# A layer step on one core: 56 instead of 48 tokens of the expert layer by row, one of its one-hots on ScalarE, and the second norm in two sets of columns

## The chip, the cores and the metric

The kernel is one program on one core of a Trainium2 chip. The metric is device time in microseconds (us), the median of repeated runs. The engines are named as the profile names them: PE (TensorE), DVE (VectorE), ACT (ScalarE), POOL (GpSimd), SP (the engine that issues the weight loads).

## The reference, cut to what matters

One layer of a decoder on 264 tokens (256 of a prompt and one each of 8 samples), all in fp32. The change lies in the second half of it, from `x1` on:

```
q   = x1 @ w_q                                  # 8 heads x 2 x 128
s1, s2 = q[:, :, 0] . keys1, q[:, :, 1] . keys2 # 128 scores each
t1, i1 = top_k(s1, 16);  t2, i2 = top_k(s2, 16)
cand = t1[:, None] + t2[None, :]                # 256 per head
top, pos = top_k(cand, 16); idx = i1 * 128 + i2 at pos
gate = softmax(top)                             # 8 x 16 = 128 experts per token
hid  = gelu(x1 . u_tab[idx])                    # 16,384 experts of 2,048 numbers
peer = sum(gate * hid * v_tab[idx])
x2   = LN(ALPHA * x1 + peer)
y    = x2 + sigmoid(x2 @ ple_gate_w) * (p @ ple_proj_w)
```

## The kernel before, in words

**Two ways through the expert layer.** A token needs 128 rows of `u_tab` and of `v_tab`. `NSP` tokens (the last ones, the samples among them) are done by row: for each, 128 rows of `uR` are gathered by an indirect DMA into a tile `ug` of 128 x 2048 (1 MiB), DVE multiplies them with the token's `x1` and sums (L1230), then 128 rows of `vR` are gathered and added with their coefficients into a sum tile `x1s` (L1240). All other tokens, `TD` = 264 - `NSP` = 216, are done densely by PE: all 16,384 experts' products with `x1` (stage U, 128 blocks of two weight halves), a gelu, a multiplication with a gate matrix that is zero where an expert was not chosen, and the sum over all experts (stage V, 8 chunks of 16 blocks).

**A block on PE.** `pair_block` (L261 to L278) takes two weight tiles of 128 x 1024 (a "half" each). A weight is split by ACT into a rounded part `whi` (`split_w`, L146) and by DVE into the rest `wlo` (L147). Per slice of 128 rows there are two matmuls: `whi` with the activations' two parts beside each other (2·TD columns, L271 or L274) and `wlo` with the first part alone (TD columns, L272). So 16 pairs make a block. The stages ahead use `col_block`, three matmuls of 264 columns per slice (L235 to L237); the change does not touch them.

**What sets the order.** All five instruction streams are written out by hand. Each half is a `tick`: the weight fetch four halves ahead is issued on SP (five `w` buffers, L135), the split three halves ahead is put on ACT and DVE (four `whi` and `wlo` buffers), the half's matmuls are issued, and then the background gets a budget of about one microsecond of DVE time (`background`). Background work is a list of generators that yield the cost of what they just issued, or a wait of n ticks; what stands earlier in the list is served first. The engines then run these streams first-in first-out, held by semaphores only. The generators here:

- `select` (L1020) finds the 16 best of each head, in three token sets t = 0, 1, 2; `select_all` (L1088) runs them and starts what follows.
- `gates` (L1152) makes the gate matrix: per group of 4 tokens POOL writes a one-hot with the gate in it, `o1` (4 x L1165), DVE writes a plain one-hot `o2` (L1166), PE multiplies the two six ticks later (`g_mm`, L1178), ACT copies the product into `gs` (L1179), SP sends `gs` to DRAM. A grid asks for 3 ticks from group to group.
- `sparse_experts` (L1194) does the tokens by row in groups `GR` of 32 and 16. One job is one gather and one DVE pass; a gather is issued one job ahead, and a grid asks for `STEP` = 4 ticks from job to job. For a group of n tokens, `x1s` first takes 128/n copies of the group's `x1` rows (L1220) and later the sum, which PE folds at the end (L1246).
- `prep` (L1305) makes the dense coefficients for V: it loads gates and products (`gl`, `al`, issued on POOL), multiplies them on DVE (L1315, L1316) and splits the result on ACT and DVE (`co`, L1324, L1325). Each chunk of 16 blocks needs four such steps; a chunk begins with `run_out`, which issues at once what is left of them.
- `Norm` (L800) gathers the second norm's sums while the last chunk of V still runs: every evacuated block (L1351, L1354) gets the tokens by row copied in (POOL, L1355) and is then treated over all 264 columns (L825, L831, L832, L841 to L844). `n2` is this norm. The projection behind it (`ple_half`, 16 blocks of `w_pg`) follows.

## Time and profile before

| | before |
|---|---|
| median of 3 runs | 2614.34 us (2608.11 to 2621.4) |
| the profiled execution | 2611.91 us, span 2610.1 us |
| PE busy | 2579.9 us (99%) |
| DVE, ACT, POOL busy | 2033.3, 1342.6, 734.4 us |
| moved by DMA | 676.77 MB |

In time, the part up to `x1` ends near 1147 us; stage U runs from there to 1850 us, V to 2495 us, the projection behind it to the end. A row of the profile names line, engine and operation, then what is written and read (`out<-in`), its shape and a count; "idle before" is time in which that engine stood still just ahead of it, with the instruction that ended the wait. A row of a timeline begins with its start and its duration in us.

### The profile page before, as it was taken

How to read it: one execution, taken by the hardware profiler on the slowest of the kernel's cores; microseconds unless marked ns; L12 is line 12 of the kernel's file. 1: busy time of each engine (PE TensorE's matmuls, PEld its weight loads, DVE VectorE, ACT ScalarE, POOL GpSimd, SP SyncE). 2: the span in 40 equal slices, each digit the busy share in tenths (PEclk: the TensorE clock that was granted, in tenths of full speed). 3: DMA queues.
4: the chain of work that ended last, by engine and by line, in shares of the span. 5: the costliest groups of instructions: out<-in, count | busy, mean ns of one | idle time of the engine just before them, and what ended most of it. 6: DMA issues, size and time to landing. Idle time of an engine off the chain costs nothing.

```text
span 2610.1 us, 48704 instructions
## 1 busy us (share of the span) xinstructions
PE 2579.9 (99%) x18967; PEld 2526.5 (97%) x18967; DVE 2033.3 (78%) x3256; ACT 1342.6 (51%) x1893; POOL 734.4 (28%) x774
## 2 busy tenths in 40 slices
PE   9999999999999999999999999999999999999999
PEld 8999999999999999999999999999999999999999
DVE  8899965556445567889998777778889799897886
ACT  5665533444334444655556655656445444444563
POOL 2232200000000010100269999883322232220100
PEclk9999999999999999999999999999999999999999
DMA  7798755656666666667778999899999999997664
GB/s 236 220 302 271 240 178 176 181 175 181 184 179 179 183 180 179 177 184 209 227 228 316 351 331 337 332 335 391 366 360 378 346 370 371 373 379 232 202 199 133
DMA packets 201399, 676.77 MB, mean 259 GB/s; under 512 B 23168, under 2 KB 60704, under 8 KB 187680
## 3 DMA queue, kind: packets, MB, share of 16 engines
q1 hardware_dynamic: 156384, 509.65, 59.9%
q0 software_dynamic: 26768, 145.43, 14.8%
q10 hardware_dynamic: 18016, 18.58, 2.0%
q8 instruction: 148, 2.42, 0.4%
q14 instruction: 83, 0.68, 0.1%
HBM read 632.67 MB, written 40.90 MB: 258 GB/s over the span
## 4 chain that ended last, share of the span: by engine, by line
PE 90%; DVE 4%; DMA 4%; issue 1%; ACT 0%; SPq 0%; POOL 0%; DVEq 0%; POOLq 0%; ACTq 0%
PE mm L271 26%; PE mm L237 15%; PE mm L235 15%; PE mm L236 15%; PE mm L272 14%; DMA w<-uT 2%; PE mm L274 2%; PE gps L1178 2%; DVE wlo L147 1%; DVE x1s L1240 1%; DMA al<-a_d 0%; DMA ug<-vR,sidx 0%; ACT whi L146 0%; DMA ug<-uR,sidx 0%; PE scr L996 0%
## 5 line engine op out<-in xcount | busy, mean ns | idle before, releaser
L147 DVE TENSOR_TENSOR wlo<-w,whi 128x1024 fp32r<-128x1024 f32 x916 | 1120.4, 1226 | 392.1 <-ACT whi L146 388.8
L146 ACT CAST whi<-w 128x1024 fp32r<-128x1024 f32 x916 | 960.2, 1050 | 797.2 <-PE mm L236 287.4
L271 PE MATMUL mm<-x,whi 128*128 128x432 f32 x1920 | 607.1, 373 | 0.7 <-ACT whi L146 0.7
L271 PE MATMUL mm<-co,whi 128*128 128x432 f32 x1920 | 601.9, 371 | 3.5 <-DVE co L1325 3.5
L237 PE MATMUL mm<-x,wlo 128*128 128x264 f32 x1920 | 549.3, 286 | 2.8 <-DVE wlo L147 2.8
L235 PE MATMUL mm<-x,whi 128*128 128x264 f32 x1920 | 549.0, 286 | 0.1
L236 PE MATMUL mm<-x,whi 128*128 128x264 f32 x1920 | 546.6, 285 | 0.0
L272 PE MATMUL mm<-x,wlo 128*128 128x216 f32 x2048 | 519.1, 264 | 7.6 <-DVE wlo L147 7.6
L272 PE MATMUL mm<-co,wlo 128*128 128x216 f32 x2048 | 518.4, 263 | 3.3 <-DVE wlo L147 3.3
L272 PEld LDWEIGHTS mm<-x,wlo 128*128 128x128 f32 x2048 | 391.4, 191 | 13.4 <-DVE wlo L147 11.3
L272 PEld LDWEIGHTS mm<-co,wlo 128*128 128x128 f32 x2048 | 390.5, 191 | 6.0 <-DVE wlo L147 4.3
L271 PEld LDWEIGHTS mm<-co,whi 128*128 128x128 f32 x1920 | 361.6, 188 | 21.9 <-DVE co L1325 5.1
L271 PEld LDWEIGHTS mm<-x,whi 128*128 128x128 f32 x1920 | 361.9, 188 | 16.5 <-ACT whi L146 0.9
L1165 POOL TENSOR_SCALAR o<-iot,slot,slot 128x128 f32<-128x128 f32 x216 | 360.2, 1676 | 24.3 <-PE gps L1178 20.7
L237 PEld LDWEIGHTS mm<-x,wlo 128*128 128x128 f32 x1920 | 361.7, 188 | 3.2 <-DVE wlo L147 3.2
L235 PEld LDWEIGHTS mm<-x,whi 128*128 128x128 f32 x1920 | 362.8, 189 | 1.8 <-issue 1.4
L236 PEld LDWEIGHTS mm<-x,whi 128*128 128x128 f32 x1920 | 362.9, 189 | 0.0
L1202 POOL DMA_INDIRECT ug<-vR,sidx x48 | 84.4, 1759 | 292.7 <-DVE x1s L1240 218.7
L833 POOL CAST r1h<-r1gbh 128x2 fp32r<-128x2 f32 x16 | 5.2, 326 | 476.3 <-PE mm L237 476.3
L1230 DVE SCALAR_TENSOR_TENSOR ug<-ug,x1s 128x2048 f32<-128x2048 f32 x48 | 109.7, 2286 | 10.8 <-DMA ug<-uR,sidx 10.8
L1240 DVE SCALAR_TENSOR_TENSOR x1s<-ug,scf,x1s 128x2048 f32<-128x2048 f32 x46 | 107.9, 2345 | 2.6 <-DMA ug<-vR,sidx 2.6
L1202 POOL DMA_INDIRECT ug<-uR,sidx x48 | 70.5, 1468 | 116.7 <-DVE ug L1230 106.0
(350 smaller groups left out, 3834.6 us busy)
## 6 DMA issues: line engine op xcount, KB each, us to landing
w<-uT SPq DMA_DIRECT2D x256, 512.0 KB
w<-vP SPq DMA_DIRECT2D x256, 512.0 KB
w<-w_in SPq DMA_DIRECT2D x240, 512.0 KB
w<-w_bc SPq DMA_DIRECT2D x32, 512.0 KB
w<-w_bs SPq DMA_DIRECT2D x32, 512.0 KB
w<-w_o SPq DMA_DIRECT2D x32, 512.0 KB
w<-w_q SPq DMA_DIRECT2D x32, 512.0 KB
w<-w_pg SPq DMA_DIRECT2D x32, 512.0 KB
```

What stands on the lines that cost most here:

```text
L146: ac.copy(hi, w)
L147: ve.tensor_tensor(lo, w, hi.bitcast(F), OP.subtract)
L235: te.matmul(ps, wh, xh[kb], start=(first and q == 0), stop=False)
L236: te.matmul(ps, wh, xl[kb], start=False, stop=False)
L237: te.matmul(ps, wl, xh[kb], start=False, stop=(last and q == n - 1))
L271: te.matmul(ps, hi[:, ws], xp[kb], start=(kb == 0), stop=False)
L272: te.matmul(ps[:, :TD], lo[:, ws], xp[kb][:, :TD], start=False, stop=False)
L274: te.matmul(ps, hi[:, ws], xp[kb], start=False, stop=True)
L1165: gp.tensor_scalar(o1[:, q], iot, slot[0][:, c], slot[2][:, c], OP.is_equal, OP.mult)
L1202: gp.indirect_dma_start(out=t, out_offset=None, in_=tab, in_offset=bass.IndirectOffsetOnAxis(ap=sidx[:, c:c + 1], axis=0))
L1230: ve.scalar_tensor_tensor(t, t, 1.0, x1s, OP.mult, OP.mult, accum_out=shid[:, c:c + 1])
L1240: ve.scalar_tensor_tensor(x1s, t, scf[:, c:c + 1], x1s, OP.mult, OP.add)
```

## The change

- `NSP` is 56, so `TD` is 208, and `GR` gets a third group of 8 tokens. `NB`, `TR` (gates kept in blocks of 32 tokens and a rest) follow: the rest is 16 tokens instead of 24.
- `o2` comes from ACT: per group four `Abs` of (slot - iota) and one `Relu` of (1 - that) over all four, where DVE had one `is_equal`.
- `sparse_experts` starts after set t = 1 and at the head of the task list, where it started after t = 0 and at its end. Jobs come every 4 ticks, but every second one (every fourth in V) after 3. `x1s` has two buffers; the next group's copies come by one DMA (`replicate`) while the present group is in its second half, and the fold is a task of its own (`folded`).
- `select` works through its one-hot search in quarters instead of halves.
- `prep` is put at the head of the list and waits 2 instead of 3 ticks between steps; the budget of a tick in V is 1.1 instead of 1.0.
- The second norm gathers only the dense columns of each block (`w` = TD). The columns of the tokens by row are done for all 16 blocks at once (`finish`, `Norm.rest`), when the last fold is through.

```diff
-NSP = 48
+NSP = 56
-GR = ((0, 32), (32, 16))
+GR = ((0, 32), (32, 16), (48, 8))
...
     class Norm:
-        def __init__(self, g_base, b_base, name, new):
+        def __init__(self, g_base, b_base, name, new, w=T):
...
-            ve.tensor_tensor(s, s, self.c, OP.subtract)
+            ve.tensor_tensor(s[:, :w], s[:, :w], self.c[:, :w], OP.subtract)
...
+        def rest(self, xs, sq):
+            w, n = self.w, T - self.w
+            ps = bank("pil")
+            te.matmul(ps[:, :n], o128, xs[:, 0], start=True, stop=True)
+            c = block("pc")[:, :n]
+            ac.copy(c, ps[:, :n])
+            yield ("w", 1)
+            ve.tensor_tensor(xs, xs, c[:, None, :].to_broadcast([128, 16, n]), OP.subtract)
...
+            ac.activation(sq, xs, AF.Square)
+            ve.tensor_reduce(self.acc[0][:, w:T], xs.rearrange("p j t -> p t j"), AX.X, OP.add)
...
+            ve.tensor_reduce(self.acc[1][:, w:T], sq.rearrange("p j t -> p t j"), AX.X, OP.add)
+            yield 1.0
+            for j in range(16):
+                while len(self.h) <= j:
+                    yield ("w", 1)
+                h, l, x = self.h[j][:, w:T], self.l[j][:, w:T], xs[:, j]
+                ac.activation(h, x, AF.Copy, scale=col(self.g, j))
+                gp.tensor_copy(self.d[j][:, w:T], x)
+                def low(h=h, l=l, x=x, j=j):
+                    ve.scalar_tensor_tensor(l, x, col(self.g, j), h.bitcast(F), OP.mult, OP.subtract)
+                soon(low)
+                yield 0.2
...
-        HH = max(1, nh // 2)
+        HH = max(1, nh // 4)
...
-            if t == 0:
-                spawn(sparse_experts())
+            if t == 1:
+                spawn(sparse_experts(), True)
...
-            ve.tensor_tensor(o2, iot[:, None, :].to_broadcast([128, 4, 128]),
-                             slot[1][:, tt:tt + 4, None].to_broadcast([128, 4, 128]), OP.is_equal)
+                ac.activation(o2[:, q], iot, AF.Abs, bias=slot[1][:, c], scale=-1.0)
+            ac.activation(o2, o2, AF.Relu, bias=1.0, scale=-1.0)
...
+        def replicate(g):
+            k0, n = GR[g]
+            t = lp.tile([128, D], F, name="x1s", tag="x1s", bufs=2)
+            gp.dma_start(out=t, in_=bass.AP(tensor=x1_d.tensor, offset=x1_d.offset + k0 * D,
+                                            ap=[[0, 128 // n], [D, n], [1, D]]))
+            return t
...
             if tab is uR and c == k0:
-                x1s = lp.tile([128, D], F, name="x1s", tag="x1s", bufs=1)
-                for q in range(128 // n):
-                    gp.dma_start(out=x1s[q * n:(q + 1) * n], in_=x1_d[ks])
-                yield ("w", 4)
+                x1s = xr
...
             get(i + 1)
-            yield grid(STEP)
+            yield grid(STEP - (i % (4 if vp else 2) == 0))
...
             if c == ECH - 1:
-                s = a[:, :T]
                 ve.tensor_tensor(a[:, :TD], a[:, :TD], a[:, TD:], OP.add)
-                gp.tensor_copy(s[:, TD:], x1sp[:, db])
-                n2.add(s)
+                n2.add(a[:, :T])
...
-            while "sparse" not in DONE:
-                tick(1.1)
-            spawn(ple_parts())
+            spawn(finish())
         co = [CO.pop(16 * c + e) for e in range(16)]
         for db in range(KB):
-            pair_block(co, v_evac(c, db), 1.0)
+            pair_block(co, v_evac(c, db), 1.1)
```

What this does to the order is seen best at three places. The first is ACT's stream in the middle of the gates (stage U), one gate group's worth of it. Before, with `as` the evacuated products, `gs` the gate matrix and `whi` the next weight:

```order
L1280 COPY as<-mm 128x216
L146 CAST whi<-w 128x1024
L1179 COPY gs<-gps 128x4x128
L1284 ACTIVATE as<-as 128x432
L1285 DMA a_d<-as 128x432
L146 CAST whi<-w 128x1024
```

And after, at the corresponding place:

```order
L1332 COPY as<-mm 128x208
L1201 ACTIVATE o_17359<-iot,slot_14374 128x128 x4
L1202 ACTIVATE o_17359<-o_17359 128x512
L146 CAST whi<-w 128x1024
L1336 ACTIVATE as<-as 128x416
L1337 DMA a_d<-as 128x416
L146 CAST whi<-w 128x1024
L1332 COPY as<-mm 128x208
L146 CAST whi<-w 128x1024
L1214 COPY gs<-gps 128x4x128
```

Five instructions per group have come onto ACT between the weight splits (the `o` tile is `o2`); no further table loads stand between them.

The second place is DVE's stream at the end of a chunk of V, 752 weight splits (L147) into the program. Before:

```order
L147 TENSOR_TENSOR wlo<-w,whi 128x1024
L1315 TENSOR_TENSOR al<-al,gl 128x4x192
L1316 TENSOR_TENSOR al<-al,gl 128x4x24
L147 TENSOR_TENSOR wlo<-w,whi 128x1024
L1351 TENSOR_TENSOR acc<-mm,acc 128x432
L1230 SCALAR_TENSOR_TENSOR ug,shid<-ug,x1s 128x2048
L1325 TENSOR_TENSOR co<-al,co 128x4x216
L147 TENSOR_TENSOR wlo<-w,whi 128x1024
L1230 SCALAR_TENSOR_TENSOR ug,shid<-ug,x1s 128x2048
L147 TENSOR_TENSOR wlo<-w,whi 128x1024
```

After, at the same count:

```order
L147 TENSOR_TENSOR wlo<-w,whi 128x1024 x2
L1403 TENSOR_TENSOR acc<-mm,acc 128x416
L1299 SCALAR_TENSOR_TENSOR x1s<-ug,scf,x1s 128x2048
L147 TENSOR_TENSOR wlo<-w,whi 128x1024 x2
L1403 TENSOR_TENSOR acc<-mm,acc 128x416
```

The chunk's last step of `prep` stood right at the chunk's end, together with two jobs by row; now the four steps stand closer together early in the chunk and are over by its end.

The third is DVE's stream in the last chunk, 869 splits in, where `Norm.rest` (L863, L867, L870) is woven between the blocks' own norm work:

```order
L1405 TENSOR_TENSOR acc<-acc 128x208
L829 TENSOR_TENSOR acc<-acc,pc 128x208
L863 TENSOR_TENSOR x1sp<-x1sp,pc 128x896
L147 TENSOR_TENSOR wlo<-w,whi 128x1024
L845 SCALAR_TENSOR_TENSOR r_28332<-acc,cpar,r_28332 128x208
L847 TENSOR_TENSOR da<-da,acc 128x208
L848 TENSOR_TENSOR dsq<-dsq 128x208
L867 TENSOR_REDUCE da<-x1sp 128x56
```

Before, the same norm instructions stood there with 264 columns, and nothing of a rest. By the same count, the first job by row stands 441 splits in (460 before) and the last 859 (820 before); the last evacuation of V is at 883 in both.

More of the change, by code (lines that the diff above doesn't have):

```diff
@@ L187, in background, with spawn @@
                 clock["credit"] -= r
-    def spawn(gen):
+    def spawn(gen, first=False):
         tk = {"gen": gen, "wait": 0}
-        tasks.append(tk)
+        tasks.insert(0 if first else len(tasks), tk)
         return tk
@@ L200, in __call__ @@
         def __call__(self, n):
-            self.t = max(self.t + n, clock["t"] + 1)
+            self.t = max(self.t + n, clock["t"])
             return ("w", self.t - clock["t"])
@@ L817, in pilot @@
             ps = bank("pil")
-            te.matmul(ps[:, :T], o128, self.s0, start=True, stop=True)
+            te.matmul(ps[:, :self.w], o128, self.s0[:, :self.w], start=True, stop=True)
             self.c = block("pc")
-            ac.copy(self.c, ps[:, :T])
+            ac.copy(self.c[:, :self.w], ps[:, :self.w])
             self.gather(self.s0)
@@ L830, in on_act @@
             def on_act():
-                ac.activation(h[:, :T], s, AF.Copy, scale=col(self.g, j))
-                ac.activation(q, s, AF.Square)
+                ac.activation(h[:, :w], s[:, :w], AF.Copy, scale=col(self.g, j))
+                ac.activation(q[:, :w], s[:, :w], AF.Square)
                 gp.tensor_copy(h[:, T:], self.gb[0][:, j])
@@ L1138, in send @@
                 src = range(lo, min(lo + m, n))
-                rows(gp, g, 0, src, m * m, 128 // m, m)
+                if len(src):
+                    rows(gp, g, 0, src, m * m, 128 // m, m)
         else:
@@ L1144, in later_rows @@
                 for h in range(PH):
-                    rows(sy, g, h * m + m - NS, range(h * NS, h * NS + NS), m * m, 1, m)
+                    rows(sy, g, h * TOPK + m - NS, range(h * NS, h * NS + NS), m * m, TOPK // m, m)
                 DONE["sent"] = True
@@ L1209, in index, with folded @@
             gp.dma_start(out=scf[:, k0:k0 + n], in_=sg_d[g])
+        def replicate(g):
[4 more added lines that the diff above has]
+            return t
+        def folded(g, acc):
+            k0, n = GR[g]
+            yield ("w", 2)
+            ps = bank("yS")
+            for db in range(KB):
+                te.matmul(ps[:, db * n:(db + 1) * n], acc[:, db * 128:(db + 1) * 128], fld[:, k0:k0 + n],
+                          start=True, stop=True)
+                if db % 4 == 3:
+                    yield ("w", 1)
+            xs = x1sp[:, :, k0:k0 + n]
+            ve.scalar_tensor_tensor(xs, xs, ALPHA, ps[:, 0:KB * n].rearrange("p (j t) -> p j t", t=n),
+                                    OP.mult, OP.add)
+            yield 0.8
+            DONE["S" + str(g)] = True
         yield ("w", 1)
@@ L1213, in sparse_experts @@
         get(0)
+        xr = replicate(0)
+        yield ("w", 4)
         grid = Grid()
+        g = 0
         for i, (tab, k0, n, c) in enumerate(jobs):
@@ L1217, in sparse_experts @@
             if tab is uR and c == k0:
-                x1s = lp.tile([128, D], F, name="x1s", tag="x1s", bufs=1)
-                for q in range(128 // n):
-                    gp.dma_start(out=x1s[q * n:(q + 1) * n], in_=x1_d[ks])
-                yield ("w", 4)
-            if i == 32:
-                while "sent" not in DONE:
+                x1s = xr
+            if tab is vR and c == k0 and g + 1 < len(GR):
+                while g + 1 == len(GR) - 1 and "sent" not in DONE:
                     yield ("w", 1)
-                index(1)
+                index(g + 1)
+                xr = replicate(g + 1)
             get(i + 1)
-            yield grid(STEP)
+            yield grid(STEP - (i % (4 if vp else 2) == 0))
             t = rows.pop(i)
@@ L1242, in sparse_experts @@
             if c == k0 + n - 1:
-                yield ("w", 2)
-                ps = bank("yS")
-                for db in range(KB):
-                    te.matmul(ps[:, db * n:(db + 1) * n], x1s[:, db * 128:(db + 1) * 128], fld[:, ks],
-                              start=True, stop=True)
-                    if db % 4 == 3:
-                        yield ("w", 1)
-                xs = x1sp[:, :, ks]
-                ve.scalar_tensor_tensor(xs, xs, ALPHA, ps[:, 0:KB * n].rearrange("p (j t) -> p j t", t=n),
-                                        OP.mult, OP.add)
-                yield 0.8
+                spawn(folded(g, x1s), True)
+                g += 1
+        while "S" + str(len(GR) - 1) not in DONE:
+            yield ("w", 1)
         DONE["sparse"] = True
@@ L1328, in prep @@
             yield 1.1
-            yield ("w", 3)
+            yield ("w", 2)
     def r2_pair(name):
@@ L1352, in f, with finish @@
             if c == ECH - 1:
-                s = a[:, :T]
                 ve.tensor_tensor(a[:, :TD], a[:, :TD], a[:, TD:], OP.add)
-                gp.tensor_copy(s[:, TD:], x1sp[:, db])
-                n2.add(s)
-        return f
+                n2.add(a[:, :T])
+        return f
+    def finish():
+        while "sparse" not in DONE or n2.acc is None:
+            yield ("w", 1)
+        spawn(ple_parts())
+        sq = lp.tile([128, D], F, name="sq", tag="ug", bufs=2)[:, 0:KB * NSP].rearrange("p (j t) -> p j t", t=NSP)
+        yield from n2.rest(x1sp, sq)
+        DONE["rest"] = True
     def residual():
@@ L1370, in ple_parts @@
         gp.dma_start(out=pi, in_=pT)
-        pp = lp.tile([128, D], R, name="pp", tag="x1s", bufs=1)[:, 0:4 * T].rearrange("p (a q t) -> p a q t", q=2, a=2)
+        pp = lp.tile([128, D], R, name="pp", tag="x1s", bufs=2)[:, 0:4 * T].rearrange("p (a q t) -> p a q t", q=2, a=2)
         yield ("w", 4)
@@ L1386, in to_v @@
         vp = ctx.enter_context(tc.tile_pool(name="vp", bufs=1))
-        t = spawn(prep(0))
+        t = spawn(prep(0), True)
         spawn(residual())
@@ L1406, in hybrid_step @@
         if c + 1 < ECH:
-            nxt = spawn(prep(c + 1))
+            nxt = spawn(prep(c + 1), True)
         else:
-            while "sparse" not in DONE:
-                tick(1.1)
-            spawn(ple_parts())
+            spawn(finish())
         co = [CO.pop(16 * c + e) for e in range(16)]
         for db in range(KB):
-            pair_block(co, v_evac(c, db), 1.0)
+            pair_block(co, v_evac(c, db), 1.1)
     def ple_half(q):
@@ L1434, in norm2 @@
     def norm2():
-        while len(n2.d) < 16:
+        while len(n2.d) < 16 or "rest" not in DONE:
             yield ("w", 1)
@@ L1442, in norm2 @@
             yield ("w", 1)
+    while len(p_h) < 2:
+        tick(1.3)
     spawn(norm2())
```

28 lines of the change are left out of this document (18 added, 10 removed).

## The prediction

> **What bounds the kernel now.** I read the page first: busy shares and the chain that ended last.
>
> ```profile
> span 2610.1 us, 48704 instructions
> PE 2579.9 (99%) x18967; PEld 2526.5 (97%) x18967; DVE 2033.3 (78%) x3256; ACT 1342.6 (51%) x1893; POOL 734.4 (28%) x774
> PE 90%; DVE 4%; DMA 4%; issue 1%; ACT 0%; SPq 0%; POOL 0%; DVEq 0%; POOLq 0%; ACTq 0%
> ```
>
> PE is the bound nearly everywhere; what makes PE's stream shorter shortens the span, as long as the others keep up. Whether they do differs by stage, so next the busy times by stage. The rows are: the part of U with gates and jobs by row together, the end of U, V with jobs by row, V without. After the length stand PE, PEld (weight loads), DVE, ACT, POOL, then clock, DMA share and GB/s.
>
> ```profile
> 1390.00:1765.00 375.00, 373.54 (x2524) 364.06 (x2524) 283.33 (x312) 218.54 (x285) 338.06 (x205) 1.00 0.91 334
> 1765.00:1850.00 85.00, 82.41 (x530) 78.83 (x529) 74.54 (x74) 56.48 (x82) 22.90 (x19) 1.00 1.00 392
> 1850.00:2337.00 487.00, 480.27 (x3107) 463.70 (x3106) 437.94 (x431) 221.56 (x217) 144.96 (x138) 1.00 0.97 367
> 2337.00:2495.00 158.00, 157.98 (x1032) 153.12 (x1031) 128.10 (x178) 77.52 (x96) 18.07 (x53) 1.00 0.74 227
> ```
>
> Three resources stand close behind PE: POOL with the gates (338 of 375 us), the DMA engines at the end of U (share 1.00), DVE in V (438 of 487 us, 90%). Last, what PE waited for in U and V (1147 to 2495 us): total, times, longest.
>
> ```profile
> PE mm L272 <- DVE wlo L147: 10.9, 13, 2.6
> PE mm L271 <- DVE co L1325: 3.5, 6, 1.4
> PE mm L271 <- ACT whi L146: 0.7, 1, 0.7
> ```
>
> So 15.1 us in 1348: PE goes at its own pace, and that pace is what the change alters.
>
> **PE's columns.** A quiet stretch of V, by starts (the second column is a modelled duration), then two matmuls of 264 columns.
>
> ```profile
> 2459.28 0.37 PE L271 MATMUL mm<-co,whi 128*128 128x432 f32 x1
> 2459.48 0.26 PE L272 MATMUL mm<-co,wlo 128*128 128x216 f32 x1
> 2459.58 0.37 PE L271 MATMUL mm<-co,whi 128*128 128x432 f32 x1
> ...
> 2460.00 0.37 PE L274 MATMUL mm<-co,whi 128*128 128x432 f32 x1
> ...
> 2464.94 0.37 PE L274 MATMUL mm<-co,whi 128*128 128x432 f32 x1
> ...
> 2503.03 0.28 PE L1423 MATMUL mm<-pp,whi 128*128 128x264 f32 x1
> 2503.15 0.28 PE L1424 MATMUL mm<-pp,whi 128*128 128x264 f32 x1
> ```
>
> From L274 to L274 is one block: 4.94 us for 16 x (432 + 216) = 10,368 columns, 0.476 ns each. The change takes 16 + 8 columns from each of 16 pairs, 384 per block: 0.183 us, times 256 blocks = 46.8 us. The bounds: start to start is 0.10 us at 216 columns, 0.12 at 264, 0.20 to 0.21 at 432. From 264 to 432 that is about 0.09 us for 168 columns, 0.54 ns each, so 53 us. If the short matmul, already at 0.10, gets no shorter, 256 of the 384 columns count: 31 us. I take 46.8, since the block is the longest thing measured.
>
> **PE's other work.** Two gate groups go (54 to 52), a third fold comes.
>
> ```profile
> L1178 PE MATMUL gps<-o,o 128*128 128x128 f32 x432 | 57.3, 276 | 0.0
> L1246 PE MATMUL yS<-fld,x1s 128*128 128x32 f32 (+1 forms) x64 | 7.8, 259 | 0.0
> ```
>
> 57.3 / 54 = 1.06 each, so -2.1; 7.8 / 2 = +3.9, the same for 8 tokens as for 32 and 16 since 16 matmuls stand in each. Sum +1.8.
>
> **ACT with the one-hots.** No `Abs` is in the trace; the nearest row is a 128 x 128 activation with a pointer operand (L632); for the `Relu` of 512, one of 432 (L1284). Then ACT's present work between 1390 and 1765 us.
>
> ```profile
> L632 ACT ACTIVATE h0t<-h0t,dexp x128: 384/392/418, 95.6 to 299.2; 128x128 f32<-128x128 f32 x128
> L1284 ACT ACTIVATE as<-as x64: 555/567/647, 1156.3 to 1846.3; 128x432 f32<-128x432 f32 x64
> L1179 ACT COPY gs<-gps 128x512 f32<-128x512 f32 x44 | 51.4, 1167 | 61.1 <-PE gps L1178 61.1
> L1280 ACT COPY as<-mm 128x216 f32<-128x216 f32 x67 | 22.5, 335 | 44.3 <-PE mm L274 44.1
> ```
>
> Per group 4 x 0.392 + 0.567 x 512/432 = 2.2 us; 44 groups make 97 us, so ACT goes from 218.5 of 375 to 316 of about 363 (87%; each of the 67 blocks is 0.18 us shorter). It fits, beside work that PE does anyway, at zero cost on the path. The cover is thin: ACT's 105 us of waiting for PE in its own order (last two rows) must shrink, or it ends as the third rival.
>
> **POOL with the gates.** POOL is the nearest to its limit. Its one-hot L1165 (minimum, median, maximum ns between 1420 and 1600 us), the DVE passes beside it, and what came of it late in U:
>
> ```profile
> L147 DVE TENSOR_TENSOR wlo<-w,whi 128x1024 fp32r<-128x1024 f32 x916 | 1120.4, 1226 | 392.1 <-ACT whi L146 388.8
> L1165 POOL TENSOR_SCALAR o<-iot,slot,slot x85: 781/1391/4927, 1419.4 to 1597.8; 128x128 f32<-128x128 f32 x85
> L1166 DVE TENSOR_TENSOR o<-iot,slot x54: 671/681/1071, 1292.3 to 1731.7; 128x512 f32<-128x512 f32 x54
> L1230 DVE SCALAR_TENSOR_TENSOR ug<-ug,x1s x48: 2277/2284/2371, 1391.3 to 2198.0; 128x2048 f32<-128x2048 f32 x48
> 1701.93 11.44 POOL L1165 TENSOR_SCALAR o<-iot,slot,slot 128x128 f32<-128x128 f32 x4
> 1729.84 1.01 POOL L1202 DMA_INDIRECT ug<-uR,sidx  x1 [0.17 <-issue]
> 1737.81 2.29 DVE L1230 SCALAR_TENSOR_TENSOR ug<-ug,x1s 128x2048 f32<-128x2048 f32 x1 [5.47 <-DMA ug<-uR,sidx]
> 1744.33 0.61 POOL L1208 DMA_DIRECT2D sidx<-sx_d  x1
> ```
>
> The same one-hot takes 0.78 to 4.93 us, so something holds POOL up. From the start of the first POOL row here to that of the last stand five groups and four gathers with hardly a pause: 42.4 us, 8.5 per group, where PE's group takes 3 halves of 2.47 and 1.06, 8.5 as well. POOL has no slack there; a gather left late, and DVE stood 5.47 us for it with the next weight splits behind it in its queue. Of the 8.5 us, 4 x 0.78 + 0.75 x 1.01 = 3.9 are POOL's own. The rest, 4.6, is about three quarters of what DVE does from SBUF to SBUF per group, 3 x 1.23 + 0.68 + 0.75 x 2.28 = 6.1, so I take DVE's passes as the cause, and three quarters as their weight. By the Trainium skill, "SBUF — State Buffer", the reading of its port diagram, a DVE instruction with two SBUF inputs and a POOL instruction that reads SBUF exclude each other for a whole instruction; the trace agrees as far as these 8.5 us tell. The change takes L1166's 0.68 us off DVE (x 3/4 = -0.51 for POOL), and puts jobs 3.5 ticks apart for 4: per group of 3 ticks 0.86 for 0.75 jobs, 0.11 x (2.28 x 3/4 + 1.01) = +0.30. POOL's group would be 8.3 us, PE's 3 x 2.38 + 1.06 = 8.2: about level again, but jobs begin 19 halves earlier, over the last selection's DVE passes, so what POOL has run ahead by then (three `o1` buffers at most) is used up sooner. I add 5 us of PE waiting, between -3 and +15.
>
> **DVE and DMA in V.** DVE's work per half hardly changes, so 437.9 us would fill 93% of 487 - 98 x 0.18 = 469 us. What goes is the pile at chunk ends (order, second place): the 3.5 us of `co` above, and part of this,
>
> ```profile
> DVE al L1315 <- DMA al<-a_d: 21.8, 6, 6.9
> ```
>
> DVE standing for a load that had not landed (6.9 us once), with weight splits queued behind it. Against it, the steps of `prep` now come 5 to 7 halves apart, about 12 to 17 us for a load to land in. I take -3 us, between -7 and +12. The bytes per half stay, so 367 GB/s becomes 381; the row at 392 held with PE running, so DMA costs nothing yet.
>
> The copies of `x1` now come as one transfer whose source leads with 4, 8 or 16 repeats:
>
> ```profile
> x1s<-x_d POOLq DMA_DIRECT2D x4, 256.0 KB, 11.8
> x1s<-x_d POOLq DMA_DIRECT2D x8, 128.0 KB, 7.4
> ```
>
> They landed in 7 to 12 us; the new ones are asked for half a group ahead, so I cost them at nothing and keep +5 us for a gather queued behind them, a wait like the 5.47 above. The Trainium skill speaks against it: "DMA: Bandwidth & Descriptors", "Rules for kernel authors", says an outermost dimension of c < 16, such as a zero-stride broadcast, keeps a transfer on at most c engines. By it the first copy has 4 engines of 16, at 392/16 GB/s each 10.7 us alone and twice that beside the weights: an estimate by which the +5 would be the value to take. No run here shows it.
>
> **The last chunk.** The rest is one pass over 896 elements, two sums of as many, 16 passes of 56; each block's own passes lose 56 of 264 columns, which I leave out. Nearest rows:
>
> ```profile
> L1325 DVE TENSOR_TENSOR co<-al,co 128x864 fp32r<-128x864 f32 x32 | 33.6, 1051 | 0.0
> L1076 DVE TENSOR_REDUCE sel<-big 128x64 f32<-128x1024 f32 x8 | 9.7, 1209 | 0.0
> L1316 DVE TENSOR_TENSOR al<-al,gl 128x96 f32<-128x96 f32 x32 | 8.0, 251 | 0.0
> ```
>
> 1.05 + 2 x 1.2 + 16 x 0.25 = 7.5 us of DVE at most, where its stretch has 30 us free (128 of 158). The last job stands 24 halves ahead of the end of V, the rest between, so all is hidden but a little: +1 us (0 to +4). If jobs slipped by more than those 24 halves (57 us), PE would wait in full.
>
> **Sum**, against the profiled 2611.9 us: -46.8 + 1.8 + 5 - 3 + 1 = -42.0, so 2569.9. The profiled run lies 2.4 us under the median of the three; I predict **2572 us** for the median.
>
> **Rivals.**
> 1. *POOL paces the gates.* If its group stays at 8.5 us, or goes to 8.8 because the jobs' 0.30 comes and the 0.51 does not, PE waits 0.3 to 0.6 us on each of the 47 groups that have jobs beside them, 14 to 28 us in place of my 5: 2581 to 2595. For it: the 5.47 us. Against: until the jobs begin POOL can run ahead of PE, as far as the three `o1` buffers let it.
> 2. *DMA is the bound from U's end on.* If 367 is V's ceiling, V's 487 us cannot shrink by its 18 us, and the end of U loses 3: 2593. Against: 392 was reached.
> 3. *ACT paces the gates; slower.* If ACT's 105 us of waiting in 44 groups (2.4 us each) stays whole, a group takes (218.5 + 97 + 105)/44 = 9.6 us for 8.2: 1.4 x 52 = 73 us, so 2645. It begins to cost once over 1.0 of the 2.4 us stays, and the result passes the time before at 1.8. Against: those waits are ACT being early, which more work fills.
> 4. *The columns are not what PE pays for.* PE could be bound by its weight loads: PEld is busy for 97% of the span, each matmul has one 128 x 128 load ahead of it, and their number stays. Then the time is 2611.9 + 1.8 + 3 + 2.4 = 2619. Against it: with the same load the pitch is 0.10, 0.12 and 0.21 us as the columns are 216, 264 and 432, so a load binds at 0.10 at most. Half of it, only the long matmul shortening, is the 31 us bound: 2588. The Trainium skill is on this rival's side: "Perfetto Trace Analysis", "Identifying the Most-Contended Engine", has weight-load busy share, not matmul busy time, tell how near PE is to its limit; by that rule 97% is a limit that the change leaves where it is.
>
> **How the numbers follow.** Forecast 0.68 (2556 to 2588 by its bounds), rival 1 0.14, 2 0.07, 3 0.05, 4 0.06, half of that in its milder form. Under 2556 would need the steep column price and fewer waits together; over 2595 only rivals 3, the hard form of 4 and the edge of 1 go: together under 0.2. So 2556 to 2595. A measurement of this kernel tells about 0.5% (13 us, 2601) from no change: faster 0.91 (forecast, 1, 2, half of 4), same 0.04 (hard 4 and stray cases of 1), slower 0.05.
>
> **What would show it.** A quiet block in V of 4.76 us; PE waits in U and V near 18 us, most of them in U's gates; L1165 with a like spread, ACT near 87% there; no `co` waits at chunk ends; the rest over before PE's last V block. Wrong would be: a block still at 4.9 us; PE waiting on `gps` operands or on `whi` throughout the gates; a late stretch in which PE waits for the second norm's columns.

## The result and the profile after

The changed kernel takes **2650.84 us** (median of 4 runs, 2645.87 to 2653.27) against 2614.18 of the kernel before on the same chip: ratio 1.0137, 95% interval 1.0106 to 1.0167. It is 1.4% slower, where 2572 us and faster was predicted. The profiled execution took 2653.27 us. Its page:

```profile
span 2651.0 us, 49042 instructions
PE 2572.5 (97%) x18985; PEld 2536.4 (96%) x18985; DVE 2032.7 (77%) x3271; ACT 1426.3 (54%) x2170; POOL 723.4 (27%) x775
PE 23%; DMA 6%; DVE 4%; issue 1%; ACT 1%; POOL 0%; ACTq 0%; DVEq 0%
```

PE is busy 7 us less than before, but the span is 41 us longer: what was saved came back as standing. The stages of before (the columns are those of the windows shown there):

```profile
1390.00:1765.00 375.00, 350.10 (x2359) 342.40 (x2358) 261.08 (x279) 275.29 (x477) 304.68 (x209) 0.98 0.90 330
1765.00:1850.00 85.00, 82.21 (x538) 80.55 (x537) 64.33 (x62) 48.37 (x70) 33.87 (x28) 0.98 0.98 373
1850.00:2337.00 487.00, 478.40 (x3147) 467.61 (x3145) 431.92 (x434) 231.59 (x244) 143.53 (x125) 1.00 0.97 364
2337.00:2495.00 158.00, 157.12 (x1054) 155.90 (x1054) 144.72 (x175) 76.53 (x88) 38.06 (x44) 1.00 0.88 327
```

In the gates' stage PE lost 25 of 375 us, where it had lost 1.5; no other engine stood near its limit there (ACT 73%, up from 58%; POOL 81%, down from 90%). So engines waited for each other. What PE, DVE and ACT waited for in U and V, 1147 to 2531 us (total, times, longest):

```profile
ACT whi L146 <- DMA w<-uT: 71.2, 22, 22.0
PE mm L274 <- DVE wlo L147: 34.4, 28, 13.5
PE mm L273 <- ACT whi L146: 19.9, 4, 17.4
DVE x1s L1299 <- DMA ug<-vR,sidx: 16.6, 1, 16.6
PE gps L1213 <- POOL o L1200: 5.0, 6, 1.6
```

PE stood 54.3 us for weight splits (11.6 before), and more than half of that is two single waits of 17.4 and 13.5. A quiet block of V, from the last matmul of one to the next:

```profile
2434.17 0.36 PE L276 MATMUL mm<-co,whi 128*128 128x416 f32 x1
2438.99 0.36 PE L276 MATMUL mm<-co,whi 128*128 128x416 f32 x1
```

4.82 us, where 4.94 stood before: 0.12 us less, not the 0.18 predicted.

To say where the time is, I add up for each block of U and V how far it exceeds the kernel's quiet block (4.93 before, 4.81 after; 0.11 us taken off for each foreign matmul inside it). The sums of this **excess**, in us, by stage; the last five columns are kernels of the experiments:

| stage | before | after | copies by rows | contiguous source | mended | mended, two groups | before, SP relieved |
|---|---|---|---|---|---|---|---|
| 1300–1390 | 3.1 | 24.7 | 15.5 | 17.0 | 7.9 | 7.2 | 1.1 |
| 1390–1765 | 3.6 | 34.2 | 27.1 | 19.6 | 8.9 | 11.5 | −0.5 |
| 1765–1850 | 1.7 | 5.6 | 7.9 | 8.3 | 4.4 | 1.6 | −0.1 |
| 1850–2340 | 9.8 | 16.1 | 19.2 | 8.0 | 20.1 | 3.4 | 9.5 |
| 2340–2520 | 0.8 | 3.4 | 3.4 | 3.4 | 9.5 | 1.0 | 0.8 |
| all from 1147 | 25.0 | 90.5 | 79.7 | 63.0 | 57.2 | 31.4 | 15.2 |

After less before: excess +65.5, quiet blocks −0.119 x 256 = −30.5, other matmuls +2.0, first block later by 1.4, from the last block to the end +2.6: +41.0, which is the difference of the spans (40.9). Of the +65.5, two blocks hold 36.3: one at 1320 us of 26.4 us, one at 1691 of 21.3.

**The block at 1320.** SP's queue, POOL's, ACT's, in that order:

```profile
1298.79 4.18 SPq L135 DMA_DIRECT2D w<-uT  x3
1308.24 0.35 SPq L1165 DMA_DIRECT2D sx_d<-ix  x1
...
1314.50 0.26 SPq L1165 DMA_DIRECT2D sg_d<-sel  x1
1316.07 27.57 SPq L135 DMA_DIRECT2D w<-uT  x7
```

```profile
1311.17 0.79 POOL L1249 DMA_DIRECT2D x1s<-x_d  x1
```

```profile
1337.13 1.04 ACT L146 CAST whi<-w 128x1024 fp32r<-128x1024 f32 x1 [22.00 <-DMA w<-uT]
```

SP asks for no weights from 1303 to 1316: it stands for `ix` and then gives out sixteen row transfers. In that gap POOL asks for the first 1 MB of copies, and the next weight tile, asked for at 1316, is used only at 1337. The transfer rates meanwhile (last two columns: mean DMA share, GB/s):

```profile
1320.00:1325.00 5.00, 0.79 (x6) 0.52 (x4) 0.00 (x0) 0.00 (x0) 1.27 (x2) 0.82 1.04 207
1325.00:1330.00 5.00, 0.00 (x0) 0.00 (x0) 0.00 (x0) 0.00 (x0) 0.00 (x0) 0.50 1.00 189
1330.00:1335.00 5.00, 0.00 (x0) 0.00 (x0) 0.00 (x0) 0.00 (x0) 0.00 (x0) 0.50 1.06 214
```

The DMA engines show as fully busy and move half of the 392 GB/s seen before.

How the transfers land says why. Each transfer reports its landing on a semaphore, a counter that the waiting engine watches, and the trace records this in sixteen steps. Of the steps of the copies (4 in front) eleven are recorded by 1318.3 us and four more at 1338.2 to 1339.4, 28 us after the request. Of the weight tile asked for at 1316, twelve come by 1321.8 and the last four at 1335.5 to 1337.0, just ahead of the split that waited for it. The second copy (8 in front) has eight steps by 1683.7 and eight at 1696.2 to 1697.5; the third (16 in front) has all sixteen at 2162.3 to 2164.4. So as many steps are late as the dimension in front counts, and the weight tile behind the first copy is late in just as many.

**The block at 1691.** POOL asks for the second group's copies and, behind them, for the rows of the next V job; then DVE:

```profile
1681.84 0.67 POOL L1249 DMA_DIRECT2D x1s<-x_d  x1
1682.81 1.63 POOL L1237 DMA_INDIRECT ug<-vR,sidx  x1 [0.30 <-issue]
```

```profile
1701.59 2.35 DVE L1299 SCALAR_TENSOR_TENSOR x1s<-ug,scf,x1s 128x2048 f32<-128x2048 f32 x1 [16.63 <-DMA ug<-vR,sidx]
```

DVE takes its work in order, so the weight splits wait 16.6 us behind that job, and PE 13.5 of them behind the splits.

### The profile page after: what moved, and what is told of

Its sections match the earlier page's. It is cut to its first block, busy times and chain, and to the rows that moved or that the text cites. A ratio compares the mean times of both kernels' runs of the same rounds, so it can differ in the third digit from the quotient of the medians.

```text
span 2651.0 us, 49042 instructions
## 1 busy us (share of the span) xinstructions
PE 2572.5 (97%) x18985; PEld 2536.4 (96%) x18985; DVE 2032.7 (77%) x3271; ACT 1426.3 (54%) x2170; POOL 723.4 (27%) x775
## 5 line engine op out<-in xcount | busy, mean ns | idle before, releaser
L147 DVE TENSOR_TENSOR wlo<-w,whi 128x1024 fp32r<-128x1024 f32 x916 | 1117.1, 1225 | 461.8 <-ACT whi L146 449.2
L273 PE MATMUL mm<-x,whi 128*128 128x416 f32 x1920 | 601.7, 373 | 19.0 <-ACT whi L146 19.0
L273 PE MATMUL mm<-co,whi 128*128 128x416 f32 x1920 | 588.4, 367 | 0.9 <-ACT whi L146 0.9
L274 PE MATMUL mm<-x,wlo 128*128 128x208 f32 x2048 | 516.5, 262 | 27.2 <-DVE wlo L147 26.8
L274 PE MATMUL mm<-co,wlo 128*128 128x208 f32 x2048 | 514.4, 261 | 7.9 <-DVE wlo L147 7.6
L274 PEld LDWEIGHTS mm<-co,wlo 128*128 128x128 f32 x2048 | 390.4, 191 | 15.2 <-DVE wlo L147 14.5
L273 PEld LDWEIGHTS mm<-x,whi 128*128 128x128 f32 x1920 | 366.0, 191 | 24.7 <-ACT whi L146 20.0
L1200 POOL TENSOR_SCALAR o<-iot,slot,slot 128x128 f32<-128x128 f32 x208 | 311.7, 1505 | 3.6 <-ACT slot L1142 1.9
L1237 POOL DMA_INDIRECT ug<-vR,sidx x56 | 101.8, 1818 | 300.8 <-DVE x1s L1299 253.5
L1237 POOL DMA_INDIRECT ug<-uR,sidx x56 | 85.5, 1527 | 227.0 <-DVE ug L1289 202.6
L1299 DVE SCALAR_TENSOR_TENSOR x1s<-ug,scf,x1s 128x2048 f32<-128x2048 f32 x53 | 124.3, 2345 | 16.7 <-DMA ug<-vR,sidx 16.6
L1289 DVE SCALAR_TENSOR_TENSOR ug<-ug,x1s 128x2048 f32<-128x2048 f32 x56 | 127.8, 2282 | 3.8 <-DMA ug<-uR,sidx 3.8
```

The costliest lines, as they stand in the source:

```text
L147: ve.tensor_tensor(lo, w, hi.bitcast(F), OP.subtract)
L273: te.matmul(ps, hi[:, ws], xp[kb], start=(kb == 0), stop=False)
L274: te.matmul(ps[:, :TD], lo[:, ws], xp[kb][:, :TD], start=False, stop=False)
L1200: gp.tensor_scalar(o1[:, q], iot, slot[0][:, c], slot[2][:, c], OP.is_equal, OP.mult)
L1237: gp.indirect_dma_start(out=t, out_offset=None, in_=tab, in_offset=bass.IndirectOffsetOnAxis(ap=sidx[:, c:c + 1], axis=0))
L1289: ve.scalar_tensor_tensor(t, t, 1.0, x1s, OP.mult, OP.mult, accum_out=shid[:, c:c + 1])
```

## The experiments

The theory after this look: `replicate` (the copies as one transfer) starves weights and gathers. Rivals: SP's row transfers and the earlier start of the jobs; ACT's one-hots; a smaller price of the columns. Each kernel is the changed one with the edit shown, unless said otherwise; 1.0137 is the ratio to come down from. The kernel before took 2611.8 to 2616.0 us in the medians beside the different runs, which stand on several chips; so where two times stem from different chips, the difference is taken from the ratios.

**Copies by rows**

```
-            gp.dma_start(out=t, in_=bass.AP(..., ap=[[0, 128 // n], [D, n], [1, D]]))
+            for q in range(128 // n):
+                gp.dma_start(out=t[q * n:(q + 1) * n], in_=x1_d[k0:k0 + n])
```

> The changed kernel, with only the copies of x1 taken back to the old form: 4, 8 or 16 transfers of 32, 16 or 8 rows in place of one transfer with a repeat in front. Main theory (the one transfer with repeats starves the weight loads): PE's two long blocks, 26.4 us at 1320 and 21.3 us at 1691 against 5.7 for their neighbours, lose their excess of 20.7 and 15.6 us, and the 3.5 us at 2165 goes: 2651 - 36 to 40, so 2611 to 2615, about the time before. Rival A (SP's sixteen row transfers, asked for just ahead of the first stall, and the earlier start of the jobs starve the weights): the first stall stays, 2632 to 2651. Rival B (the many small stalls of the gates, not the copies, carry the loss): 2640 or more.

2639.07, ratio 1.0094 (1.0068 to 1.0121): 12 us, a third of what was expected. The block at 1320 falls from 20.7 to 7.8 over; the one at 1691 keeps 14.3, with DVE again standing for the same gather (14.5 us). The old form was not what kept the kernel before out of this.

**Different rows**

```
+            gp.dma_start(out=t, in_=bass.AP(tensor=uR.tensor, offset=uR.offset,
+                                            ap=[[(n + 1) * D, 128 // n], [D, n], [1, D]]))
```

> The changed kernel, its one transfer kept in shape (4, 8 or 16 in front, then 32, 16 or 8 rows of 8 KB), but the source is 128 different rows of uR in place of the same rows repeated; the experts' input is wrong by this, the amount of work is not. Theory K (a short leading dimension ties the transfer to 4 or 8 DMA engines, and the weight tiles, which need all, wait for those): as the changed kernel, 2643 to 2653, 8 KB packets in a train of some 20 us again. Theory H (several engines read the same row of memory at once, and this slows every packet): 8 KB packets back at 0.31 us, no weight packet at 0.31, and both long stalls shrink to 5 us or less each: 2612 to 2625.

2653.41, ratio 1.0150 (1.0123 to 1.0178): nothing changes, so reading the same rows at once is not the cause. H falls, K stands.

**One transfer in the kernel before**

> The kernel before, with only the copies of x1 changed: one transfer with the repeat in front for each of its two groups (4 and 8 in front). If the transfer by itself does the harm, each of the two costs PE 10 to 20 us, the jobs' own wait for it comes on top: 2630 to 2655. If it only does harm together with SP's row transfers and the earlier start: 2612 to 2620.

2624.78, ratio 1.0027 (1.0010 to 1.0044), so +7 by the ratio and +9 by the medians: between the two. The transfer costs something by itself (blocks of 8.7 us over at 1323 and 7.0 at 1770), but far from 36: the rest needs the new surroundings.

**Fewer columns in the kernel before**

```
+                wd = 2 * TD if kb == 0 else 2 * TD - 16
...
-                te.matmul(ps[:, :TD], lo[:, ws], xp[kb][:, :TD], start=False, stop=False)
+                te.matmul(ps[:, :TD - 8], lo[:, ws], xp[kb][:, :TD - 8], start=False, stop=False)
```

> The kernel before, with 16 columns less in 15 of 16 long matmuls and 8 less in all short ones of each block of U and V (the left-out columns are not computed): 368 columns less per block, nothing else changed. By the mean price of the prediction, 0.476 ns a column: 256 x 0.175 = 44.8 us, 2569. By the block of the changed kernel (4.81 us against 4.93): 256 x 0.11 = 29 us, 2585. If other waits fill the gap at once, as in the changed kernel's gates: 2590 to 2605.

2603.64, ratio 0.9962 (0.9947 to 0.9977): 12 us of gain. The quiet block falls to 4.83 (0.10 for 368 columns, so 0.27 ns a column, not 0.476), and the excess grows from 25.0 to 38.4, so half of the 26 us comes back as waits. Neither price of a column gave the time by itself.

**The gather ahead of the copies**

```
+            get(i + 1)
             if tab is vR and c == k0 and g + 1 < len(GR):
                 index(g + 1)
                 xr = replicate(g + 1)
-            get(i + 1)
```

> The changed kernel (2651) with one order turned round at the start of each group's V jobs: the gather of the next job's rows is asked for ahead of the index and the copies of the next group, not behind them. Nothing else, the one transfer with repeats stays. Theory (the gather queued behind 1 MB of copies held DVE 16.6 us in L1299, and the weight splits behind it held PE): the long block at 1691 loses its 15.6 us, most of the 3.5 at 2165 stays, the one at 1320 stays: 2632 to 2637. Rival (the volume or the form of the transfer does it wherever it stands): 2645 to 2653, the wait then falls on weights or on the following gather.

2648.46, ratio 1.0139 (1.0104 to 1.0174): the rival's side. The 15.6 us become 4.6 and 8.7 in two blocks at that place. The order on the queue says who waits, not how long.

**Spread copies.** By rows, and those of the second and third group one or two per job, behind the job's gather.

```
...
+            for f in todo[:g + 1]:
+                f()
+            todo = todo[g + 1:]
```

> The changed kernel with the copies in small transfers as in the run of copies by rows (2639), but for the second and third group each asked for behind the job's own gather, one of 16 rows or two of 8 rows per job, over eight jobs; the first group's four stay together at the start. If queueing behind the copies is the cause of the blocks at 1672 (14.3 us) and 2147 (8.7): 2639 - 14 to 23, so 2616 to 2625. If those waits come from the total load of the DMA engines: above 2632.

2634.86, ratio 1.0094 (1.0057 to 1.0131), the same ratio as the copies by rows: no gain is shown, and the time is on the side of the second expectation. Two blocks from 1684 us on are still 10.4 us over, and what stands there is another queue. SP of this kernel:

```profile
1675.62 9.44 SPq L135 DMA_DIRECT2D w<-uT  x4
1691.80 0.33 SPq L1205 DMA_DIRECT2D g_d<-gs  x1
1692.21 19.88 SPq L135 DMA_DIRECT2D w<-uT  x6
```

SP stands 6.7 us for a store of gate sums (`gs`, the gate matrix), which are late because POOL's one-hots were late, and weights are asked for behind it. The copies were only the largest of several waits that end in the weights.

**Early start**

```
-            if t == 1:
-                spawn(sparse_experts(), True)
+            if t == 0:
+                spawn(sparse_experts())
```

On the spread copies:

> The kernel of spread copies, with the jobs started where the kernel before starts them: after the first selection and behind the tasks that are there, so that the first gather and copies are asked for some 10 us ahead of SP's sixteen row transfers and not right behind them. Theory (copies and the 13 us in which SP asks for no weights fall together because the start was moved): the first stall of 7.8 us goes, 4 to 9 us below the kernel of spread copies. Rival (the start does not matter, or jobs beside the selections cost DVE more): within 3 us of it, or above.

2626.28, ratio 1.0058 (1.0039 to 1.0076): 9 us less, the size expected but not for its reason, since the stall near 1311 stays (9.5). The gain is in the gates: their excess falls from 21.1 to 11.2 us.

And alone, on the changed kernel:

> The changed kernel with only the start of the jobs put back: after the first selection, behind the tasks that are there, in place of after the second and ahead of them. The one transfer with repeats stays. Theory (the earlier, preferred jobs take DVE and POOL from the gates, and their first copies fall on SP's rows): as between the two kernels with spread copies, 9 us, and up to 20 if the first long block goes too: 2631 to 2642. Rival (the start costs nothing, only the copies' form does): 2647 to 2653.

2629.46, ratio 1.0062 (1.0043 to 1.0082): 21 us, the largest effect of any single edit that keeps the computation. The first U job comes at 1393 us (1391 in the kernel before), where the preferred jobs had it at 1358, over the selections and the gates. The first long block falls from 20.7 to 9.3 and the gates' excess from 34.2 to 13.8 with the one transfer still there; 7 us are lost again at the end, where PE waits for `pp`. The edit moves the start and the place in the list together, so their shares are not known.

**SP's rows spread**

```
...
+            for h in range(PH):
+                defer(4 + h, lambda h=h: later_rows(h))
```

> The changed kernel (2651) with SP's sixteen row transfers given out two per half from four halves later on, in place of all at once two halves after the second selection; copies and start of the jobs stay. Theory (SP asks for no weights for 13 us around these rows, and the copies then meet empty weight buffers): the first long block, 20.7 us over, loses a third to a half, 2639 to 2646. Rival (the copies alone starve the weights): 2648 to 2653, the first block as it was.

2638.69, ratio 1.0103 (1.0083 to 1.0123): 12 us by the medians, 9 by the ratios, the theory's lower edge. The first long block falls from 20.7 to 8.7 with the copies untouched. So copies and SP's gap are both needed for its full length; each, taken away, leaves 8 to 9. The gap alone does no harm in the kernel before: there SP asks for no weights from 1305 to 1321 us, and no block near it is over by more than 2 us.

**A contiguous source.** The counterpart of the different rows: same table, same 1 MB, no short dimension in front.

```
+            gp.dma_start(out=t, in_=bass.AP(tensor=uR.tensor, offset=uR.offset,
+                                            ap=[[D, 128], [1, D]]))
```

> The changed kernel (2651), its one transfer reading 128 rows of uR that lie one behind the other, with no short dimension in front (the source of the earlier run with different rows, but for the leading 4, 8, 16; experts' input wrong, amount of work the same). Theory K (the short leading dimension ties the transfer to as many DMA engines): the copies land in a third of the time, the first long block falls from 20.7 to 8 us over or less, 2636 to 2642. Rival (1 MB ahead of the weights does it, whatever its shape): 2648 to 2654.

2626.30, ratio 1.0069 (1.0047 to 1.0092), below its band: 21 us less than the run with different rows by the ratios, by the source's shape alone, and 18 less than the changed kernel. While it lands:

```profile
1315.00:1320.00 5.00, 4.05 (x26) 3.49 (x24) 3.15 (x12) 0.00 (x0) 4.68 (x5) 1.00 0.96 350
1320.00:1325.00 5.00, 0.71 (x1) 0.29 (x1) 0.72 (x1) 1.80 (x3) 0.00 (x0) 0.67 1.00 407
```

407 GB/s where the changed kernel had 207, with a share near 1 both times. All sixteen steps of the first copy come at 1316.3 to 1318.2 us, 8.6 us after its request. The first long block falls to 9.4 over, the one at 1691 goes (1.0), and DVE's longest wait for a gather of V is 3.9 us. K holds: a short leading dimension costs about 20 us here.

**One-hots back on DVE**, on the spread copies:

> The kernel of spread copies, with the second one-hots back on DVE (one is_equal of 512 elements, 0.68 us) in place of ACT's Abs and Relu (1.9 us a group). If ACT's one-hots are what makes the small stalls of the gates (some 12 us of blocks over their pitch between 1374 and 1660): 6 to 12 us below the kernel of spread copies. If POOL, held up by gathers that wait for DVE, makes them: the same to 5 us above it, since DVE's 0.68 us a group comes back.

2651.23, ratio 1.0160 (1.0124 to 1.0195): 16 us above, against both expectations. The gates' excess hardly moves (19.2 for 21.1), but the gates end at 1817 us in place of 1763, and the first chunk's coefficients then come late: one block at 1860 is 15.9 us over, PE standing for `co`. So ACT's one-hots do not pace the gates; in this kernel they keep them ahead.

**`pi` and `pp` earlier**, on the early start: `finish` spawns `ple_parts` ahead of its wait.

> The kernel of spread copies and early start (2626), with the loads and splits of the last stage's own input (tiles pi and pp) spawned at the start of the last chunk in place of behind the last job. There PE waited 7.2 us for pp after its last V block, and the stretch from the last V block to the end was 126 us against 116 to 118 elsewhere. If that wait is the whole of it: 2616 to 2620. If the rest of the second norm is late as well, the wait moves there: 2623 to 2628.

2620.38, ratio 1.0019 (1.0009 to 1.0030): 6 us by the medians, at the edge of its band, and 10 by the ratios.

**Mended: SP relieved too.** Rows spread, and the stores of gate sums issued by ACT:

```
-                defer(8, lambda gs=gs, b0=b0: sy.dma_start(out=g_d[b0] if b0 < NB else gr_d, in_=gs))
...
+        if end is not None:
+            ac.dma_start(out=end, in_=gs)
```

> The kernel with the earlier spawn of pi and pp, and two waits taken from SP's queue besides: the sixteen row transfers go out two per half, and the stores of gate sums are issued by ACT right behind the copy that fills them, so that no weight request stands behind either. Theory (SP standing for rows and gate sums makes the blocks at 1311 and 1747, 9.5 and 8.1 us over): 10 to 16 us below it, 2602 to 2610, faster than before (2612 to 2616) by 0.2 to 0.5%. Rival (those blocks come from the copies and late one-hots themselves): within 4 us of it.

2611.31, ratio 0.9987 (0.9975 to 0.9999): 9 us, just short of the band, and level with the kernel before. 39.5 us of the changed kernel's time are undone; 39 still stand to the prediction.

**Mended, two groups.** The third group's jobs are left out (8 tokens' experts are not computed).

> The mended kernel (2611: spread copies, early start, SP's rows spread, gate sums stored by ACT), with the sixteen jobs of the third group left out, so the experts of its 8 tokens are not computed; everything else, the narrow blocks and the second norm's last pass included, stays. Theory (in V the other engines are so near their limit that sixteen more jobs of 2.3 us of DVE and 1 MB each cost nearly what the narrow blocks save): the 30 us by which V's blocks and the last chunk exceed their pitch fall to the 10 of the kernel before, 2588 to 2597. Rival (the jobs are covered, the narrow blocks meet another limit): 2604 or more.

2590.03, ratio 0.9928 (0.9907 to 0.9949): 15 us by the ratios, 21 by the medians, for sixteen jobs and their copies. V and the last chunk, with the third group (first fence) and without:

```profile
1850.00:2337.00 487.00, 474.64 (x3123) 463.66 (x3121) 428.65 (x432) 219.97 (x217) 143.72 (x140) 1.00 0.98 361
2337.00:2495.00 158.00, 152.00 (x1004) 149.07 (x1005) 147.97 (x197) 75.55 (x99) 40.80 (x55) 1.00 0.86 311
```

```profile
1850.00:2337.00 487.00, 485.66 (x3233) 480.70 (x3232) 436.14 (x439) 227.91 (x224) 130.05 (x122) 1.00 0.97 362
2337.00:2470.00 133.00, 132.87 (x883) 131.25 (x882) 114.39 (x178) 71.72 (x106) 29.40 (x49) 1.00 0.71 220
```

With 362 GB/s and a share of 0.97 PE still runs 485.7 of 487 us, so this rate alone does not hold PE up. With the third group, DVE is at 94% of the last stretch (148 of 158) and PE loses 6 us of it; without, 86% and nothing.

The loss is mostly not under the sixteen jobs, which run from 2318 us on: from 2300 to 2450 the mended kernel's blocks exceed their pitch by 2.5 us in all. About 11 us lie from 2150 to 2250, while the third group's copies are asked for (2149 to 2224), and 8.6 from 2450 on, where the last jobs and the rest of the second norm stand beside the last blocks. The first of these stretches, with the third group and without:

```profile
2145.00:2250.00 105.00, 97.66 (x625) 92.94 (x625) 85.74 (x84) 44.03 (x45) 37.26 (x43) 1.00 0.99 335
2145.00:2250.00 105.00, 105.00 (x699) 104.28 (x698) 94.53 (x91) 48.31 (x48) 33.76 (x31) 1.00 0.99 375
```

ACT stood 49.8 us for weights there, 18.5 without the group. These copies are transfers of 8 rows. In the run of copies by rows, such transfers land in two parts again (asked for at 2139.1 us: eight steps by 2144.6, eight from 2149.0 to 2151.2), where those of 16 rows land in one (asked for at 1663.8: all from 1666.3 to 1667.2). Whether the 8 rows or the volume of the copies costs the 11 us was not separated.

**SP relieved, in the kernel before**

> The kernel before (2615) with SP relieved in the same way as in the mended kernel: the sixteen row transfers two per half from four halves later on, the gate sums stored by ACT. If SP's waits are covered in the kernel before (the blocks there exceed their pitch by 1 to 2 us in these places): 2611 to 2616. If the mended kernel's gain is SP's alone, and not the change's: 2604 to 2608, and the change is worth nothing even when mended.

2604.75, ratio 0.9972 (0.9956 to 0.9988), the rival's side: the lowest ratio of all versions that compute everything, and without the change. Its interval overlaps that of the mended kernel, so no gain from the change is shown even there.

**And ACT's one-hots with it**

> The kernel before with SP relieved as in the run beside it, and ACT's Abs and Relu for the second one-hots in place of DVE's is_equal; 48 tokens by row, blocks as before. If ACT paces the gates (third rival): above the run beside it, by up to 70 us. If ACT has room and DVE's 0.68 us a group helped POOL and the jobs: 3 to 10 us below it. If both are covered: the same within 3 us.

2610.70, ratio 1.0000 (0.9987 to 1.0013): 6 us above the run beside it. The part that helps the changed kernel costs this one a little; the third rival's 70 us are not there, and from 1390 to 1765 us PE is busy for 375.0 of 375 us.

## Why the prediction was wrong, point by point

- **The step that failed is `replicate`, "I cost them at nothing and keep +5 us".** The rows behind that, copies landing in 7 to 12 us, were of transfers of 128 and 256 KB without the short dimension in front, and they said nothing of who else waits meanwhile. The first copy landed 28 us after its request, and the dimension in front cost about 20 us here (the contiguous source against the different rows), 7 to 9 in the kernel before. The rule of the Trainium skill quoted there ("DMA: Bandwidth & Descriptors", "Rules for kernel authors": an outermost dimension of c < 16 keeps a transfer on at most c engines) was on the right side; the trace agrees, in that as many of a copy's sixteen landing steps come late as its leading dimension counts. Its estimate of twice 10.7 us for the first copy stands against those 28.
- **The start of the jobs was not priced as a move.** That "jobs begin 19 halves earlier" entered the sum only through POOL's `o1` buffers, in a +5 with −3 to +15. It cost 20 to 21 us alone. The preferred jobs also came ahead of the gates' tasks, and the first copies fell beside SP's sixteen rows; how much of the cost is due to each is not shown. SP's queue, which the change moved the copies against, was not read at all.
- **The columns** gave −30.5 us of quiet blocks, not −46.8. The failed term is the price of a column: 0.476 ns is the block's length over its columns, but the 384 columns taken off were worth 0.31 ns each. The two widths inside a block would not have told it either: start to start is 99 ns at 216 columns and 208 at 432, so 0.50 ns a column. The bound of 31 was right, though not for its reason: both matmuls got shorter, by some 3 ns each. Why columns at the margin cost less than the mean is open.
- **The third group was counted as one fold, +3.9 us.** Its jobs and copies had no term of their own in V ("DVE's work per half hardly changes"). In the mended kernel the two-group run puts them at 15 to 21 us, the greater part while its copies are asked for and at the end of V. In the changed kernel it is probably less: there V's blocks are 19.5 us over, 8.9 more than before.
- **The rivals.** POOL pacing the gates was partly right (stands for `gps` of 5.0 us, and SP's store behind late one-hots), but the 28 us of its hard form need the start too. DMA with 367 GB/s as V's ceiling is refuted by the two-group run (375 GB/s from 2145 to 2250 us with PE never standing); but slow transfers, not the rate, did hold the weights up. ACT pacing the gates is refuted: these are its rows in the gates' stage, after the line of POOL's one-hots,

```profile
L1200 POOL TENSOR_SCALAR o<-iot,slot,slot 128x128 f32<-128x128 f32 x169 | 254.2, 1510 | 2.6 <-ACT slot L1142 1.1
L1201 ACT ACTIVATE o<-iot,slot 128x128 f32<-128x128 f32 x165 | 52.9, 397 | 4.0 <-ACT as L1336 4.0
L1202 ACT ACTIVATE o<-o 128x512 f32<-128x512 f32 x42 | 26.6, 632 | 1.3
```

  79.5 us for 42 groups, 1.9 each, under the 2.2 estimated. Of the fourth, only the milder form's size came true.
- **The last chunk.** The rest of the second norm is not over before the last V block: PE's last matmul of V starts at 2533 us, the last pass of the rest at 2541. It could not be, since its sixteenth pass waits in the program for the sixteenth block. From the last block to the end it is 118.2 us, 2.6 more than before; with the 2.6 us of excess in the last stage this is 5 where +1 (0 to +4) stood.
- **Right:** PE's `co` waits at the ends of V's chunks are gone, and DVE's `al` waits fell from 21.8 us to 1.1. Yet the excess from 1850 to 2340 us rose from 9.8 to 16.1 where −3 (−7 to +12) stood.

From 2651 back to 2572, by the path of these runs: copies, start, `pi`/`pp` and SP 39, the third group 15 to 21, the columns 16, together 70 to 76 of 79. The steps are not independent (by the ratios, the start alone gives 20, the copies' shape alone 18, SP's rows alone 9, on the same long blocks), so the split of the 39 is not settled. Not tried: copies without a short leading dimension in the mended kernel, whose third group still has it; they need `x1` stored 128 rows deep for each group.

## What to carry to other kernels

Price a merged transfer by its access pattern and by what stands behind it, not by how fast its pieces landed. When a change moves a task, read every in-order queue at the new place, above all the one that asks for the weights: here a gap of 13 us in SP's requests, a megabyte on POOL's queue and DVE's order turned small delays into 20 us of PE. And measure the price of a few columns by leaving them out: neither the mean of the block nor the difference of two far widths gave it, while the run with fewer columns came near (0.27 ns against 0.31).

## What the runs showed of the hardware

- A transfer with 4 or 8 in front landed in two parts: four or eight of its sixteen steps came 12 to 20 us behind the others; with 16 in front, or a contiguous source of 128 rows, all came within 2.5 us. While the one with 4 ran, the large packets took twice as long: in the changed kernel around 1320 to 1335 us a median of 0.62 us for 8 KB and 0.31 to 0.33 for the weights' 4 KB, with the contiguous source 0.31 and 0.16. The DMA share read 1.04 and 1.00, at 207 and 407 GB/s. A share of 1.00 did not mean full speed here. Why the weights' packets slow down too is open.
- The granted TensorE clock fell to 0.50 in the first long stand and was back at 1.00 some 5.5 us after PE resumed (PE resumed at 1338.2 us; 0.50 up to 1343.7, 1.00 from there), so the long stand cost more than its length. The Trainium skill, "TensorE: Matmul & The Clock Gate", "What's actually happening", has the array at half clock after an idle window of some 3.4 us; the trace agrees as to the half.
- Sixteen row transfers of 0.5 KB took SP mostly 0.3 us each to issue. With the wait ahead of them and the stores of gate sums behind late producers they cost the kernel before 7 us (2611.77 against 2604.75), though none of its blocks there was more than 2 us over.
